# Gated recurrence: the in-chunk attention of 32-token groups as 32x32 blocks in four partition strips

## The chip, the cores and the metric

The kernel runs on one core of a Trainium2 chip. The metric is the device time of one execution in microseconds (us), lower is better. The engines are named as in the profile: PE (TensorE, matmuls), PEld (its weight loads), DVE (VectorE), ACT (ScalarE), POOL (GpSimd) and SP (SyncE, which starts the DMA transfers).

## The reference

One transformer block over 512 tokens of width 1024. A norm and one wide projection feed three branches: sparse attention with a learned index, a gated linear recurrence, and latent attention. Their outputs are gated, summed and projected, and a feed-forward part follows. The change is in the recurrence (4 heads, 128 keys and 128 values each, a decay per token and key), which the reference computes chunk by chunk like this, with `lfc` the logarithm of the decays:

```python
def step(state, xs):
    qc, kc, vc, lfc = xs
    b = jnp.cumsum(lfc, axis=2)
    o_inter = jnp.einsum('bhck,bhkv->bhcv', qc * jnp.exp(b), state)
    diff = b[:, :, :, None, :] - b[:, :, None, :, :]
    decay = jnp.exp(jnp.where(causal[None, None, :, :, None], diff, NEG_BIG))
    attn = jnp.einsum('bhtk,bhsk,bhtsk->bhts', qc, kc, decay)
    o_intra = jnp.einsum('bhts,bhsv->bhtv', attn, vc)
    b_last = b[:, :, -1:, :]
    new_state = (jnp.exp(b_last[:, :, 0, :])[..., None] * state
                 + jnp.einsum('bhsk,bhsv->bhkv', kc * jnp.exp(b_last - b), vc))
    return new_state, o_inter + o_intra
```

So a query at token t meets a key at token s <= t with the product of the decays between the two.

## The kernel before

The kernel is written as a plan. Calls such as `PE.matmul` or `V.tensor_mul` only record an instruction; `Plan.run` then orders all of them by a list schedule over the five engines, with a cost for each (`Plan.cost`), a latency between engines, an extra 500 ns ahead of a PE instruction that waits for another engine (`SLACK`), and with limits on how many tiles of a kind may be alive. Tiles are drawn from classes of slots: `g` has 37 slots of 128x512 floats, `bank` the 8 banks of PSUM. Each engine runs its own list in that order and waits for nothing but the data and the slots. A change of one instruction can therefore move others anywhere. All instructions carry the line of the emitting call, L322 (L323 after), so they are told apart by tile names.

The large projections work on float32 split into two float32r parts. They are long rows of matmuls of 128x512: `hT_hi` and `hT_lo` (the two parts of the normed input, transposed) against `whi` and `wlo`. ACT casts each weight tile `raw` to `whi`, DVE forms `wlo` from the difference. SP issues the transfers of the weights in program order. While the recurrence is computed, the list of PE alternates its blocks with such rows, for the projections of the next heads and for the gates of the branches; DVE and ACT work beside it on the bias of the sparse attention, which is chosen by a tree of selections (`mux<-bits,mux` and the like).

`hgrn_pair` computes the recurrence for two heads; it is called twice. The kernel takes chunks of 128 tokens, 4 per head. The attention tile `at` (128 keys x 4 chunks x 128 queries) is built by levels. First the diagonal, from a full 128x128 product per chunk (`pd`) times the identity. Then level hh = 1, 2, 4, ... 64: queries in the upper half of each group of 2 hh tokens meet keys in its lower half, `qT` and `kT` having been multiplied by the decays up to the middle (`tt` holds products of decays over ever longer stretches). Up to hh = 16 a level takes one 128x64 product per chunk, of which a predicated copy with the mask `ci` takes the right entries into `at`. For hh = 32 and 64 there are only narrow matmuls with outputs at their own partitions, which ACT copies into `at`. Then the keys are transposed (`kn`), the states summed (`S`), the output is formed (`bi` are the values), normed (`rb` on POOL), gated (`og`), transposed and split into `ob_hi` and `ob_lo`.

At the start of the program x is normed (`jk` on ACT with its sum of squares, `r` on POOL), transposed on PE, and cast to `hT_hi`; the first projections run row tile by row tile. A mask `cm` comes from the constants through `cw`.

Of the kernel before, what the change touches and what calls it, by code (L numbers as in the profile page):

```python
# [48 lines left out]
def _consts():  # L49
    f = np.zeros((128, 512 + 32), np.float32)  # L50
    p = np.arange(128)
    f[:, 384:512] = np.where(p[None, :] <= p[:, None], 0.0, NEG)
    f[:, 512:544] = np.array([float.fromhex(v) for v in INV_FREQ], np.float32)[None, :]
    lv = np.zeros((128, 7, 64), np.int32)
    for n in range(7):
        h = 1 << n
        s, t = p[:, None], p[p % (2 * h) >= h][None, :]
        lv[:, n] = (s // (2 * h) == t // (2 * h)) & (s % (2 * h) < h)
    return f, lv.reshape(128, 448)


class Buf:
    """A tile of the plan: one slot of its class, from its first write to its last access."""

# [7 lines left out]
class View:  # L72
    """A slice of a Buf: the elements it covers, and how to cut the slice out of the real tile."""

# [68 lines left out]
class Plan:  # L143
    """Records the instructions, then emits them in the order of a list schedule over the engines."""

# [180 lines left out]
def block_kernel(ctx: ExitStack, tc: tile.TileContext, x, positions, w_in, w_up_a, w_up_b, w_up_c, w_out, mla_q_norm,  # L326
# [25 lines left out]
    def const(shape, dt=F32, name="c"):  # L352
        v = plan.tile(nm("const"), shape, dt, name)
        slots[v.buf.cls] = [(cpool, v.buf.cls)]
        v.buf.left = 1
        return v
# [8 lines left out]

# [1 line left out]
    xt = []  # L367
# [21 lines left out]

# [1 line left out]
    class W:  # L391
        pass

    def unit(segs, kt, width, tag=""):
        """segs: (source AP [kt*128, n], column in the unit). -> hi, lo [128, kt, width]"""
        w = W()
# [39 lines left out]
    def rstd(m, n, name="r"):  # L436
        """m ** -0.5, [128, n]"""
        r = st(n, name)
        P.tensor_tensor(r, m, mhalf[:, 0:n], op=ALU.pow)
        return r  # L440

    def rms2(ss, name):
        """1/sqrt(ss[0] + ss[1] + eps)"""
        m = st(1, "ms")
        V.scalar_tensor_tensor(m, ss[:, 0:1], EPS, ss[:, 1:2], op0=ALU.add, op1=ALU.add)
        return rstd(m, 1, name)
# [9 lines left out]

# [1 line left out]
    hT = (plan.tile("hT", (8, 512), F32R, "hT_hi"), plan.tile("hT", (8, 512), F32R, "hT_lo"))  # L458

    def norm_rows(src, gain, dst, t, r=None, plain=None):  # L460
        """src: two [128, 512] halves of a row tile; transposed into columns t of dst"""
        if r is None:
# [20 lines left out]

# [1 line left out]
    va = const((4, 128,), F32, "va")  # L485
# [22 lines left out]
    def two_parts(hi, los, pt, tt):  # L508
        """pt: 64 rows twice -> hi; their low part, over or under zeros"""
        A.copy(hi[:, tt], pt)  # L510
        for e, lo in enumerate(los):
            a, b = (0, 64) if e == 0 else (64, 128)
            V.tensor_sub(lo[:, tt].part(a, b), pt.part(a, b), f32(hi[:, tt]).part(a, b))
# [58 lines left out]
    SP.dma_start(invf, consts_f[:, 512:544])  # L572
    ci = const((7, 64), I8, "ci")
    cw = g((128, 7, 64), I32, "cw")
    SP.dma_start(cw.rearrange("p a b -> p (a b)"), consts_i)
    A.copy(ci, cw)
    pos_i = const((4,), I32, "pos_i")
    SP.dma_start(pos_i, positions[0].rearrange("(a p) -> p a", p=128))
# [14 lines left out]
    rows_group([(src(C_AV, 128), 0), (src(C_IK, 72), 128), (src(C_KPE, 64), 200)], 264, put1)  # L593
# [1 line left out]
    pos_f = const((4,), F32, "pos_f")  # L595
# [17 lines left out]
    V.tensor_scalar(cs, cs, -2.0, 1.0, op0=ALU.mult, op1=ALU.add)  # L613
    # the lower bound: a softmax over the depth (one layer), its running sum less its first term
    lbe = const((4,), F32, "lbe")
# [21 lines left out]
    def rope(dst, a, heads, t):  # L637
        """a, dst: [128, heads, 64]"""
        c = cs[:, t:t + 1].to_broadcast([128, heads, 32]) if heads > 1 else cs[:, t:t + 1]
# [34 lines left out]

# [1 line left out]
    iqT = []  # L676
# [38 lines left out]
    def bias_unit(parts, heads):  # L715
        """rel_bias[bucket] by a tree of selections on the bits of the bucket; parts: (block, first column)"""
        n = sum(128 * (i + 1) for i, _ in parts)
# [58 lines left out]
    background(bias_unit, [(3, 0)], range(4))  # L776
# [1 line left out]
    SC_C = float(np.float32(192 ** -0.5))  # L778
# [45 lines left out]

# [1 line left out]
    def soft(p, i, addend=None):  # L826
        """softmax of the rows in PSUM (+ addend), transposed: [128 keys, block, 128 rows]"""
        S = 128 * (i + 1)
# [21 lines left out]
    def attend(h, logits, addend, value, dst):  # L850
        """softmax(logits + addend) @ value, transposed, in two parts"""
        ot = bank("ot")
# [24 lines left out]

# [1 line left out]
    fT, kT, qT = {}, {}, {}  # L879
# [26 lines left out]
    def hgrn_pair(hs):  # L906
        qp, at, tt_ = {}, {}, {}
        for h in hs:
            at[h] = g((128, 4, 128), name="at")
            pd = bank("t", (128, 4, 128))  # L910
            for c in range(4):
                cc = slice(c * 128, (c + 1) * 128)
                PE.matmul(pd[:, c], kT[h][:, cc], qT[h][:, cc], start=True, stop=True)
            V.tensor_mul(at[h], pd, ident.rearrange("p (a c) -> p a c", a=1).to_broadcast([128, 4, 128]))
            qp[h] = qT[h]
# [11 lines left out]
        for lv in range(7):  # L927
            hh = 1 << lv
            for h in hs:
                pl = bank("t", (128, 4, 64))  # L930
                if hh >= 32:
                    for c in range(4):
                        for s in range(0, 128, 2 * hh):
                            m = 128 * c + s
                            PE.matmul(pl[:, c, 0:hh].part(s, s + hh), kT[h][:, m:m + hh], qp[h][:, m + hh:m + 2 * hh],
                                      start=True, stop=True)
                    for s in range(0, 128, 2 * hh):
                        A.copy(at[h][:, :, s + hh:s + 2 * hh].part(s, s + hh), pl[:, :, 0:hh].part(s, s + hh))
                for c in range(4 if hh < 32 else 0):
                    cc = slice(c * 128, (c + 1) * 128)  # L940
                    q2 = qp[h][:, cc].rearrange("p (n two e) -> p n two e", two=2, e=hh)[:, :, 1]
                    PE.matmul(pl[:, c], kT[h][:, cc], q2, start=True, stop=True)
                if hh < 32:
                    a2 = at[h].rearrange("p c (n two e) -> p c n two e", two=2, e=hh)[:, :, :, 1]
                    m2 = ci[:, lv:lv + 1].to_broadcast([128, 4, 64]).rearrange("p c (n e) -> p c n e", e=hh)
                    V.copy_predicated(a2, m2, pl.rearrange("p c (n e) -> p c n e", e=hh))
                if hh == 1:
                    tv = fT[h].rearrange("p (n two) -> p n two", two=2)
                else:
                    o = 512 - 1024 // hh  # L950
                    tv = tt_[h][:, o:o + 512 // hh].rearrange("p (n two) -> p n two", two=2)
# [52 lines left out]

# [1 line left out]
    aqT = []  # L1006
# [13 lines left out]

# [1 line left out]
    mixed = [None] * 8  # L1022
# [38 lines left out]

# [1 line left out]
    mx = [(o8(name="mxh"), o8(name="mxl")) for _ in range(2)]  # L1063
# [6 lines left out]
    def acc8(hi_of, lo_of, wsrc, nk, tail):  # L1070
        """banks[half][t] = rows x columns; the last `tail` units row tile by row tile"""
        us = nk // 2
# [37 lines left out]

# [1 line left out]
    act = []  # L1112
# [13 lines left out]
    for f in range(2):  # L1126
        ffn_mm(f, [slice(0, 256)])
    # column blocks in pairs by Winograd's seven products: (block, next) x (halves of the sum) x (halves of the rows)
    lo_t, hi_t, ka, kb = slice(0, 256), slice(256, 512), slice(0, 4), slice(4, 8)

    def sums():
        """-> the four sums of blocks of h, in two parts"""
        y = [[hf[t][:, 4 * k:4 * k + 4] for t in range(2)] for k in range(2)]
# [165 lines left out]
```

## Time and profile before

| what | value |
| --- | --- |
| runs, device time | 920.32, 922.41, 922.94 us (median 922.41) |
| profiled execution, span from first to last instruction | 919.2 us |
| mean granted clock of PE | 0.995 |
| busy: PE, PEld, DVE, ACT, POOL | 904.9, 794.1, 704.6, 513.2, 19.7 us |
| share of the chain that ended last: PE, DMA, DVE, ACT | 89%, 4%, 3%, 2% |

The profile is of one execution, and its span is 3.2 us below the median of the runs; durations and starts below are of that execution. Matmuls are pipelined, so the record of one is longer than the time from its start to the next start. The busy time of an engine counts overlapped stretches once.

### The profile page before, as it was taken

How to read it: one execution, taken by the hardware profiler on the slowest of the kernel's cores; microseconds unless marked ns; L12 is line 12 of the kernel's file. 1: busy time of each engine (PE TensorE's matmuls, PEld its weight loads, DVE VectorE, ACT ScalarE, POOL GpSimd, SP SyncE). 2: the span in 40 equal slices, each digit the busy share in tenths (PEclk: the TensorE clock that was granted, in tenths of full speed). 3: DMA queues.
4: the chain of work that ended last, by engine and by line, in shares of the span. 5: the costliest groups of instructions: out<-in, count | busy, mean ns of one | idle time of the engine just before them, and what ended most of it. 6: DMA issues, size and time to landing. Idle time of an engine off the chain costs nothing.

```text
span 919.2 us, 14038 instructions
## 1 busy us (share of the span) xinstructions
PE 904.9 (98%) x5294; PEld 794.1 (86%) x5294; DVE 704.6 (77%) x1432; ACT 513.2 (56%) x958; POOL 19.7 (2%) x27
## 2 busy tenths in 40 slices
PE   8999999999999999999999999999999999999996
PEld 7998878888888888887888878999999999988885
DVE  5576999998989999999454437979998899844205
ACT  5656684494638699698932326645454545543103
POOL 1000000000111000000000000000000000000000
PEclk8999999999999999999999999999999999999999
DMA  8333122331111322324014371333334333643102
GB/s 265 86 92 98 47 70 66 95 92 47 46 58 45 105 92 75 109 92 117 23 56 128 121 221 48 96 90 92 93 93 137 93 92 116 184 138 105 56 1 91
DMA packets 76804, 86.64 MB, mean 94 GB/s; under 512 B 8257, under 2 KB 63809, under 8 KB 76737
## 3 DMA queue, kind: packets, MB, share of 16 engines
q1 hardware_dynamic: 76736, 85.76, 31.1%
q8 instruction: 41, 0.67, 0.3%
q14 instruction: 27, 0.21, 0.1%
HBM read 83.64 MB, written 2.10 MB: 93 GB/s over the span
## 4 chain that ended last, share of the span: by engine, by line
PE 89%; DMA 4%; DVE 3%; ACT 2%; issue 1%; SPq 0%; POOL 0%; POOLq 0%; ACTq 0%
PE ps L322 89%; DVE wlo L322 1%; DMA raw<-in_w_ffn_up 1%; ACT whi L322 1%; DMA x2b<-in_x 1%; DMA raw<-in_w_in 1%; DMA cw<-in_consts_f 1%; DMA raw<-in_w_out 1%; SPq L322 0%; DVE qpT L322 0%; ACT qpT L322 0%; ACT jk L322 0%; DVE qpr L322 0%; ACT hT_hi L322 0%; ACT L322 0%
## 5 line engine op out<-in xcount | busy, mean ns | idle before, releaser
L322 DVE TENSOR_TENSOR wlo<-raw,whi 128x1024 fp32r<-128x1024 f32 (+3 forms) x115 | 133.3, 1179 | 66.4 <-ACT whi L322 43.3
L322 ACT CAST whi<-raw 128x1024 fp32r<-128x1024 f32 (+3 forms) x115 | 114.8, 1015 | 90.6 <-PE ps L322 29.3
L322 PE MATMUL ps<-hT_hi,whi 128*128 128x512 f32 x328 | 130.2, 397 | 0.0
L322 PE MATMUL ps<-hT_lo,whi 128*128 128x512 f32 x328 | 130.1, 398 | 0.0
L322 PE MATMUL ps<-hT_hi,wlo 128*128 128x512 f32 x328 | 129.8, 397 | 0.0
L322 ACT ACTIVATE mux<-bucket,rb,rbd 128x512 f32<-128x512 f32 (+1 forms) x157 | 105.8, 744 | 6.4 <-DVE bucket L322 6.1
L322 DVE COPY_PREDICATED mux<-bits,mux 128x512 f32<-128x512 int8 x150 | 104.6, 751 | 0.5 <-ACT mux L322 0.5
L322 PE MATMUL ps<-tl,sh 128*128 128x256 f32 x288 | 81.5, 283 | 0.0
L322 PE MATMUL ps<-th,sl 128*128 128x256 f32 x288 | 81.5, 283 | 0.0
L322 PE MATMUL ps<-th,sh 128*128 128x256 f32 x288 | 81.5, 283 | 0.0
L322 ACT CAST sh<-sf 128x512 fp32r<-128x512 f32 x72 | 44.2, 621 | 51.4 <-DVE sf L322 29.1
L322 PEld LDWEIGHTS ps<-hT_lo,whi 128*128 128x128 f32 x328 | 61.8, 188 | 11.8
L322 PEld LDWEIGHTS ps<-hT_hi,wlo 128*128 128x128 f32 x328 | 61.7, 188 | 11.7 <-issue 0.2
L322 PEld LDWEIGHTS ps<-hT_hi,whi 128*128 128x128 f32 x328 | 61.7, 188 | 11.7
L322 PE MATMUL ps<-whi,ah 128*128 128x512 f32 x176 | 68.5, 389 | 0.0
L322 PE MATMUL ps<-wlo,ah 128*128 128x512 f32 x176 | 68.5, 389 | 0.0
L322 PE MATMUL ps<-whi,al 128*128 128x512 f32 x176 | 68.5, 389 | 0.0
L322 PE MATMUL ps<-h_hi,sl 128*128 128x256 f32 x216 | 61.1, 283 | 0.0
L322 PE MATMUL ps<-h_lo,sh 128*128 128x256 f32 x216 | 61.1, 283 | 0.0
L322 PE MATMUL ps<-h_hi,sh 128*128 128x256 f32 x216 | 61.1, 283 | 0.0
L322 PE MATMUL ps<-whi,hT_hi 128*128 128x512 f32 (+3 forms) x160 | 54.4, 346 | 1.1 <-ACT hT_hi L322 1.1
L322 PEld LDWEIGHTS ps<-th,sh 128*128 128x128 f32 x288 | 55.3, 192 | 0.0
(310 smaller groups left out, 2157.0 us busy)
## 6 DMA issues: line engine op xcount, KB each, us to landing
raw<-in_w_in SPq DMA_DIRECT2D x51, 512.0 KB, 4.3
raw<-in_w_ffn_down SPq DMA_DIRECT2D x22, 512.0 KB, 4.4
raw<-in_w_ffn_gate SPq DMA_DIRECT2D x18, 512.0 KB, 3.8
raw<-in_w_ffn_up SPq DMA_DIRECT2D x18, 512.0 KB, 4.2
raw<-in_w_out SPq DMA_DIRECT2D x8, 512.0 KB, 4.6
raw<-in_w_up_c SPq DMA_DIRECT2D x4, 512.0 KB, 3.6
raw<-in_w_up_b SPq DMA_DIRECT2D x4, 512.0 KB, 3.5
raw<-in_w_up_a SPq DMA_DIRECT2D x4, 512.0 KB, 3.8
```

Source lines behind the costliest of these rows:

```text
L322: getattr(real[e], method)(*[fix(v) for v in a], **{n: fix(v) for n, v in k.items()})
```

## The change

The levels 1 to 16 and the diagonal stay within groups of 32 tokens. After the change their products are made as 32x32 blocks (32x16 for the levels): per chunk four matmuls with 32 weight columns, each into its own strip of 32 partitions of a compact tile `ac` (32 keys in each of the four strips x 4 chunks x 32 queries). The diagonal product, the predicated copies and the mask `ci` (128x80 instead of 128x448 constants) work on `ac`, at a quarter of the width. After level 16 four ACT copies of 32x128 expand `ac` into the diagonal blocks of `at`, which POOL has set to zero. At hh = 64 the outputs of the chunks alternate between the two halves of the partitions, and two ACT copies take the place of one. A small identity `id32` is made at the start by four ACT copies. Comments and docstrings are taken out too.

```diff
--- before
+++ after
-    lv = np.zeros((128, 7, 64), np.int32)
-    for n in range(7):
+    lv = np.zeros((128, 5, 16), np.int32)
+    q = np.arange(32)
+    for n in range(5):
         h = 1 << n
-        s, t = p[:, None], p[p % (2 * h) >= h][None, :]
+        s, t = p[:, None] % 32, q[q % (2 * h) >= h][None, :]
         lv[:, n] = (s // (2 * h) == t // (2 * h)) & (s % (2 * h) < h)
-    return f, lv.reshape(128, 448)
+    return f, lv.reshape(128, 80)
...
-    ci = const((7, 64), I8, "ci")
-    cw = g((128, 7, 64), I32, "cw")
+    ci = const((5, 16), I8, "ci")
+    cw = g((128, 5, 16), I32, "cw")
     SP.dma_start(cw.rearrange("p a b -> p (a b)"), consts_i)
     A.copy(ci, cw)
+    id32 = const((1, 32), F32, "id32")
+    for i in range(4):
+        A.copy(id32[:, 0].part(32 * i, 32 * i + 32), ident[:, 32 * i:32 * i + 32].part(32 * i, 32 * i + 32))
...
     def hgrn_pair(hs):
-        qp, at, tt_ = {}, {}, {}
+        qp, at, ac, tt_ = {}, {}, {}, {}
         for h in hs:
+
             at[h] = g((128, 4, 128), name="at")
-            pd = bank("t", (128, 4, 128))
+            P.memset(at[h], 0.0)
+            ac[h] = g((128, 4, 32), name="ac")
+            pd = bank("t", (128, 4, 32))
             for c in range(4):
-                cc = slice(c * 128, (c + 1) * 128)
-                PE.matmul(pd[:, c], kT[h][:, cc], qT[h][:, cc], start=True, stop=True)
-            V.tensor_mul(at[h], pd, ident.rearrange("p (a c) -> p a c", a=1).to_broadcast([128, 4, 128]))
+                for i in range(4):
+                    m = 128 * c + 32 * i
+                    PE.matmul(pd[:, c].part(32 * i, 32 * i + 32), kT[h][:, m:m + 32], qT[h][:, m:m + 32], start=True,
+                              stop=True)
+            V.tensor_mul(ac[h], pd, id32.to_broadcast([128, 4, 32]))
...
             hh = 1 << lv
             for h in hs:
-                pl = bank("t", (128, 4, 64))
-                if hh >= 32:
+                pl = bank("t", (128, 4, 16 if hh < 32 else 64))
+                if hh == 64:
                     for c in range(4):
-                        for s in range(0, 128, 2 * hh):
+                        s, m = 64 * (c % 2), 128 * c
+                        PE.matmul(pl[:, c].part(s, s + 64), kT[h][:, m:m + 64], qp[h][:, m + 64:m + 128], start=True,
+                                  stop=True)
+                    for e in range(2):
+                        A.copy(at[h][:, e:4:2, 64:128].part(0, 64), pl[:, e:4:2].part(64 * e, 64 * e + 64))
+                elif hh == 32:
+                    for c in range(4):
+                        for s in (0, 64):
                             m = 128 * c + s
-                            PE.matmul(pl[:, c, 0:hh].part(s, s + hh), kT[h][:, m:m + hh], qp[h][:, m + hh:m + 2 * hh],
+                            PE.matmul(pl[:, c, 0:32].part(s, s + 32), kT[h][:, m:m + 32], qp[h][:, m + 32:m + 64],
                                       start=True, stop=True)
-                    for s in range(0, 128, 2 * hh):
-                        A.copy(at[h][:, :, s + hh:s + 2 * hh].part(s, s + hh), pl[:, :, 0:hh].part(s, s + hh))
-                for c in range(4 if hh < 32 else 0):
-                    cc = slice(c * 128, (c + 1) * 128)
-                    q2 = qp[h][:, cc].rearrange("p (n two e) -> p n two e", two=2, e=hh)[:, :, 1]
-                    PE.matmul(pl[:, c], kT[h][:, cc], q2, start=True, stop=True)
-                if hh < 32:
-                    a2 = at[h].rearrange("p c (n two e) -> p c n two e", two=2, e=hh)[:, :, :, 1]
-                    m2 = ci[:, lv:lv + 1].to_broadcast([128, 4, 64]).rearrange("p c (n e) -> p c n e", e=hh)
+                    for s in (0, 64):
+                        A.copy(at[h][:, :, s + 32:s + 64].part(s, s + 32), pl[:, :, 0:32].part(s, s + 32))
+                else:
+                    for c in range(4):
+                        for i in range(4):
+                            m = 128 * c + 32 * i
+                            q2 = qp[h][:, m:m + 32].rearrange("p (n two e) -> p n two e", two=2, e=hh)[:, :, 1]
+                            PE.matmul(pl[:, c].part(32 * i, 32 * i + 32), kT[h][:, m:m + 32], q2, start=True, stop=True)
+                    a2 = ac[h].rearrange("p c (n two e) -> p c n two e", two=2, e=hh)[:, :, :, 1]
+                    m2 = ci[:, lv:lv + 1].to_broadcast([128, 4, 16]).rearrange("p c (n e) -> p c n e", e=hh)
                     V.copy_predicated(a2, m2, pl.rearrange("p c (n e) -> p c n e", e=hh))
+                    if hh == 16:
+                        for i in range(4):
+                            ii = slice(32 * i, 32 * i + 32)
+                            A.copy(at[h][:, :, ii].part(32 * i, 32 * i + 32), ac[h].part(32 * i, 32 * i + 32))
...
```

The order of PE, at the first blocks of the first pair of heads (`ps<-qT,kT` is a block, with its count of matmuls; the other rows are the stream of a projection). Before:

```order
L322 MATMUL ps_2472<-qT_2461,kT_2361 128x128 x4
L322 MATMUL ps_2463<-hT_hi_137,wlo_2359 128x512
L322 MATMUL ps_2463<-hT_hi_137,whi_2342 128x512
L322 MATMUL ps_2463<-hT_lo_145,whi_2342 128x512
L322 MATMUL ps_2463<-hT_hi_137,wlo_2359 128x512
L322 MATMUL ps_2463<-hT_hi_137,whi_2342 128x512
L322 MATMUL ps_2463<-hT_lo_145,whi_2342 128x512
L322 MATMUL ps_2497<-qT_2403,kT_2315 128x64 x4
```

And after, at the same place:

```order
L323 MATMUL ps_2497<-qT_2483,kT_2374 32x32 x16
L323 MATMUL ps_2488<-hT_hi_156,wlo_2372 128x512
L323 MATMUL ps_2488<-hT_hi_156,whi_2355 128x512
L323 MATMUL ps_2488<-hT_lo_169,whi_2355 128x512
L323 MATMUL ps_2488<-hT_hi_156,wlo_2372 128x512
L323 MATMUL ps_2530<-qT_2416,kT_2328 32x16 x16
L323 MATMUL ps_2488<-hT_hi_156,whi_2355 128x512
L323 MATMUL ps_2488<-hT_lo_169,whi_2355 128x512
L323 MATMUL ps_2488<-hT_hi_156,wlo_2372 128x512
L323 MATMUL ps_2488<-hT_hi_156,whi_2355 128x512
L323 MATMUL ps_2488<-hT_lo_169,whi_2355 128x512
L323 MATMUL ps_2488<-hT_hi_156,wlo_2372 128x512
```

A block has 16 matmuls of 32 columns where it had 4 of 128, and the rows of the stream between the blocks are dealt out anew.

The order of ACT at the start of the program, before:

```order
L322 ACT_TABLE_LOAD
L322 ACTIVATE jk_104,ss_105<-xa_80 128x512
L322 ACTIVATE jk_114,ss_105<-xb_84 128x512
L322 CAST whi_128<-raw_95 128x768
L322 CAST hT_hi_137<-ps_130 128x4x128
L322 CAST whi_128<-raw_100 128x768
L322 CAST hT_hi_137<-ps_139 128x4x128
```

And after:

```order
L323 ACT_TABLE_LOAD
L323 COPY id_91_93<-ident_78 32x32 x4
L323 ACTIVATE jk_113,ss_114<-xa_80 128x512
L323 ACTIVATE jk_125,ss_114<-xb_84 128x512
L323 CAST whi_141<-raw_101 128x768
L323 CAST whi_141<-raw_109 128x768
L323 CAST hT_hi_156<-ps_143 128x4x128
L323 CAST hT_hi_156<-ps_151 128x4x128
```

The copies of the identity stand at the head, and both casts of `whi` stand ahead of the first `hT_hi`.

The order of DVE at the first levels of the first pair, before (the two heads have `at_2476` and `at_2489`):

```order
L322 COPY_PREDICATED at_2489<-ci_297,ps_2506 128x256
L322 TENSOR_TENSOR qT_2461<-qT_2461,fT_2352 128x256
L322 TENSOR_TENSOR kT_2361<-kT_2361,fT_2352 128x256
L322 COPY_PREDICATED mux_2445<-bits_2120,mux_2474 128x512
L322 COPY_PREDICATED at_2476<-ci_297,ps_2527 128x128x2
L322 TENSOR_TENSOR qT_2403<-qT_2403,tt_2325 128x128x2
L322 TENSOR_TENSOR kT_2315<-kT_2315,tt_2325 128x128x2
L322 COPY_PREDICATED at_2489<-ci_297,ps_2542 128x128x2
L322 TENSOR_TENSOR qT_2461<-qT_2461,tt_2380 128x128x2
L322 TENSOR_TENSOR kT_2361<-kT_2361,tt_2380 128x128x2
```

And after (`ac_2504` and `ac_2589`):

```order
L323 COPY_PREDICATED ac_2589<-ci_305,ps_2559 128x64
L323 COPY_PREDICATED ac_2504<-ci_305,ps_2582 128x32x2
L323 TENSOR_TENSOR qT_2416<-qT_2416,tt_2338 128x128x2
L323 TENSOR_TENSOR kT_2328<-kT_2328,tt_2338 128x128x2
L323 COPY_PREDICATED mux_2444<-bits_2133,mux_2458 128x512
L323 COPY_PREDICATED ac_2589<-ci_305,ps_2611 128x32x2
L323 TENSOR_TENSOR qT_2483<-qT_2483,tt_2393 128x128x2
L323 TENSOR_TENSOR kT_2374<-kT_2374,tt_2393 128x128x2
```

The predicated copies are of a quarter of the width, and a selection of the bias (`mux`) now stands between the two heads here.

## Rows read from the trace of the kernel before

**Rows 1.** The page's first line and its part 1.

```profile
span 919.2 us, 14038 instructions
...
PE 904.9 (98%) x5294; PEld 794.1 (86%) x5294; DVE 704.6 (77%) x1432; ACT 513.2 (56%) x958; POOL 19.7 (2%) x27
```

**Rows 2.** Busy us by stretch: PE, PEld, DVE, ACT, POOL; clock, DMA share, GB/s.

```profile
209.00:303.00 94.00, 93.97 (x636) 80.60 (x635) 83.92 (x187) 54.42 (x111) 9.55 (x4) 1.00 0.20 57
303.00:430.00 127.00, 127.00 (x565) 105.20 (x564) 125.71 (x219) 105.07 (x157) 0.00 (x0) 1.00 0.29 88
```

**Rows 3.** Whom PE waits for, 26 to 520 us: total, times, longest.

```profile
PE ps L322 <- ACT kz L322: 0.6, 1, 0.6
```

**Rows 4.** Timeline of PE around a diagonal or level block: start, duration.

```profile
213.18 0.39 PE L322 MATMUL ps<-hT_hi,whi 128*128 128x512 f32 x1
213.41 0.39 PE L322 MATMUL ps<-hT_lo,whi 128*128 128x512 f32 x1
213.64 1.00 PE L322 MATMUL ps<-qT,kT 128*128 128x64 f32 x8
214.44 0.48 PE L322 MATMUL ps<-hT_hi,wlo 128*128 128x512 f32 x1
214.76 0.39 PE L322 MATMUL ps<-hT_hi,whi 128*128 128x512 f32 x1
```

**Rows 5.** Timeline of PE around a block of level 32 (two strips).

```profile
231.58 0.40 PE L322 MATMUL ps<-hT_hi,wlo 128*128 128x512 f32 x1
231.90 0.45 PE L322 MATMUL ps<-qT,kT 128*32 128x32 f32 x16
232.28 0.50 PE L322 MATMUL ps<-hT_hi,whi 128*128 128x512 f32 x1
232.62 0.39 PE L322 MATMUL ps<-hT_lo,whi 128*128 128x512 f32 x1
232.85 0.40 PE L322 MATMUL ps<-hT_hi,wlo 128*128 128x512 f32 x1
```

**Rows 6.** Groups by form, PE, 195 to 303 us.

```profile
L322 PE MATMUL ps<-qT,kT 128*32 128x32 f32 x64 | 1.8, 199 | 0.0
```

**Rows 7.** Timeline of PE, a block of level 64 (one half strip).

```profile
237.32 0.68 PE L322 MATMUL ps<-qT,kT 128*64 128x64 f32 x8
```

**Rows 8.** Groups by form, DVE, 195 to 303 us: busy, mean ns.

```profile
L322 DVE COPY_PREDICATED mux<-bits,mux 128x512 f32<-128x512 int8 x48 | 34.0, 747 | 0.0
...
L322 DVE COPY_PREDICATED at<-ci,ps 128x256 f32<-128x256 int8 x20 | 11.1, 556 | 5.3 <-PE ps L322 5.3
...
L322 DVE TENSOR_TENSOR at<-ps,ident 128x512 f32<-128x512 f32 x4 | 2.8, 694 | 0.0
...
L322 DVE TENSOR_TENSOR tt<-tt 128x64 f32<-128x64 f32 x4 | 0.9, 223 | 0.0
```

**Rows 9.** Timeline of DVE in the levels.

```profile
227.62 0.44 DVE L322 COPY_PREDICATED at<-ci,ps 128x256 f32<-128x256 int8 x1 [0.16 <-PE ps L322]
227.96 0.42 DVE L322 TENSOR_TENSOR qT<-qT,tt 128x256 f32<-128x256 f32 x1
```

**Rows 10.** Groups by form, ACT, 195 to 303 us.

```profile
L322 ACT COPY at<-ps 32x128 f32<-32x128 f32 x8 | 2.0, 256 | 7.4 <-PE ps L322 7.3
```

**Rows 11.** Timeline of PE at the start (two stretches).

```profile
11.75 0.69 PE L322 MATMUL ps<-whi,hT_lo 128*128 128x384 f32 x1
...
25.48 0.44 PE L322 MATMUL ps<-whi,hT_hi 128*128 128x384 f32 x1 [0.22 <-ACT hT_hi L322]
```

**Rows 12.** Timeline of ACT at the start.

```profile
10.49 0.83 ACT L322 CAST whi<-raw 128x768 fp32r<-128x768 f32 x1
```

**Rows 13.** The chain that ended last, at the start: start, us.

```profile
15.20 6.58 DMA cw<-in_consts_f
...
24.94 0.49 ACT hT_hi L322
```

**Rows 14.** Groups by form, POOL.

```profile
L322 POOL MEMSET ident<- 128x128 f32 x1 | 0.2, 204 | 0.3 <-POOLq L1288 0.3
```

## The prediction

> **What bounds the kernel now.** I read the page's first part, then the busy time by stretch, then what TensorE waits for, and only then single blocks. On the page TensorE is busy for 904.9 of 919.2 us [rows 1]. The recurrence is the stretch from 209 to 303 us: TensorE is busy for 93.97 of its 94 us, VectorE for 83.9 and ScalarE for 54.4; in the 127 us behind it TensorE is busy throughout [rows 2]. Between 26 and 520 us the longest wait of TensorE sums to 0.6 us [rows 3]. So inside this stretch the queue of TensorE is the clock: the blocks of the recurrence stand between projection matmuls ("stream matmuls", 128x512), and a block costs what the stream is held up by it.
>
> The profiled span is 919.2 us and the median of the runs 922.41, 3.2 above it. I make the sum against the span's stretches and take it from the median.
>
> **What a block costs now.** The start of one stream matmul to the next is 0.23 us (213.18 to 213.41). From 213.18 to 214.76 there are three of them and one wide block, so the block costs 1.58 - 0.69 = 0.89 us [rows 4]. It has four matmuls, 8 passes in the trace, since each float32 matmul is run twice. 24 blocks are of this kind: four diagonal ones (128 rows wide instead of 64; I take them at the same price, their weights being as wide) and 20 of levels 1 to 16.
>
> **What a block costs after.** It becomes 16 matmuls, 32 passes, each with 32 columns of weights, into four strips of partitions. The trace has no block in four strips, but one in two: the level of 32, with 8 matmuls and 16 passes. From 231.58 to 232.85 there are three stream matmuls and this block: 1.27 - 0.69 = 0.58 us [rows 5]. One pass of it takes 199 ns [rows 6] and all 16 take 0.45 us, so passes follow one another by (0.45 - 0.20)/15 = 16.7 ns; about 0.58 - 16 x 0.0167 = 0.31 us is fixed, the price of going to narrow tiles and back. Against it the half-tile block of level 64, whose matmuls all use the same half, takes 0.68 us for only 8 passes [rows 7]. I read this as two strips running side by side: in the trace a pair of passes, one in each strip, comes every 33 ns.
>
> The bounds of a block of 32 passes are then:
> - four strips side by side, a set of four every 33 ns: 8 x 0.033 + 0.31 = 0.58 us;
> - two at a time as now, 16.7 ns apart: 32 x 0.0167 + 0.31 = 0.84 us;
> - no overlap, each pass as long as one strip needs in rows 5, 33 ns: 0.31 + 32 x 0.033 = 1.37 us.
>
> I take the first. In rows 5 a strip is free again every 33 ns, and nothing in the rows is shared by two strips. That gives 24 x (0.89 - 0.58) = 7.4 us. Level 64 puts its outputs on alternating halves; if its 0.68 us falls to the 0.45 of the two-strip block, that is 4 x 0.23 = 0.9 us. Sum: **8.3 us** off TensorE.
>
> The Trainium skill, page "TensorEngine Tiling (Array Packing)", section "Instruction Overhead", speaks against this: each matmul has about 60 cycles of overhead, and a tiling factor should not be taken from a dimension that is already small. An estimate by it at 2.4 GHz is 25 ns a pass, 0.31 + 32 x 0.025 = 1.11 us a block, 24 x 0.22 = 5.3 us slower. The 16.7 ns of rows 5 disagree with it for two strips; no run here shows four.
>
> **VectorE.** 20 predicated copies go from 256 to 64 columns: 556 ns busy on average, the next op 0.34 us behind its start [rows 8, 9]; an op of 64 columns is 223 ns busy against 0.42 us for one of 256, so each gives back about 0.2 us: 4 us. Four masked products of 694 ns go to a quarter of the width, 0.4 each: 1.6 us. VectorE doesn't set the end here, so this is worth nothing by itself. But the order of after draws eight more mux selections (0.75 us each [rows 8]), one leaf and four steps of bias preparation into the recurrence, some 7 us, and as many stream matmuls stay there as before (217 and 218 by the order). VectorE then has 83.9 - 5.6 + 7 = 85.3 us of busy time in a stretch of 94 - 8.3 = 85.7. That ends of ops run beside the next op's start makes it less tight: with each op at the start-to-start time of its kind, as 0.34 us for the copy of 256 columns [rows 9], I add up 78 us from the first masked product to the last output, where TensorE has 90 - 8 = 82 (first block at 213, end at 303). So VectorE still fits, with little to spare; between nothing and half of the 8.3 us given back I put **1 us** of stalls into the sum, by rows 3, where TensorE did not wait.
>
> **ScalarE.** Sixteen copies of 32x128 come in (256 ns each [rows 10], 4.1 us) and four copies of 64x256 become eight of half the size. ScalarE has 54.4 of 94 us [rows 2], so they are hidden. But the copies of one head wait for the last predicated copy, and behind them in ScalarE's queue stand the casts of the next weights and the copies that free the projection's PSUM: if level 16 is late, these are late, and next the stream. That is part of the 1 us.
>
> **GpSimd.** Four memsets of 128x512 are new. One of 128x128 takes 204 ns [rows 14], so by size four of 128x512 are at most 3.3 us. Three are ahead of the first norm's power, where GpSimd, busy for 19.7 us of the whole span [rows 1], waits for VectorE; the fourth is behind it. Hidden by that wait; if it were not there, the first norm would be up to 2.5 us later. They hold four of 37 slots of the g class until the recurrence, and yet the order of TensorE doesn't differ between the start and the recurrence, so no cost.
>
> **Start.** The four identity copies stand at the head of ScalarE, which idles for the first x tile there. The order of ScalarE then puts the second whi cast (0.83 us [rows 12]) ahead of the first hT_hi cast, so the third matmul, at 11.75 us now [rows 11], starts about 1 us later. In return the casts of the third row tile stand ahead of cm, whose wait for the constants' transfer (15.20 + 6.58 = 21.78 us) is on the chain and delays hT_hi to 24.94 [rows 13], where TensorE stalls and restarts at 25.48 [rows 11]: up to 1 us comes back. Net **0**, bounds -1 and +1.7. The smaller mask (40 KB for 224) is on that queue too, and hidden.
>
> **Sum.** -7.4 - 0.9 + 1 + 0 = -7.3, so 922.4 - 7.3 = **about 915.1 us**.
>
> **Rivals.**
> - *Strips overlap in pairs only*, so the change hardly does what it says: 0.84 us a block, 24 x 0.05 + 0.9 = 2.1 us: 920.3, no change to be told. For it: only pairs are seen in rows 5. Against: nothing in the row says that two is the limit. 0.14.
> - *VectorE or ScalarE becomes the bound of the recurrence.* VectorE's 85.3 of 85.7 us speak for it, and that a stall of TensorE is not made up later since it is full until 430 us. Against: rows 9 show VectorE waiting for TensorE in the levels. If half of the 8.3 is given back: 918.3. 0.20.
> - *The other side: 32 passes in four strips go one after another*, as a queue of matmuls that can't start them faster would have it: 33 ns each is 1.37 us a block and 24 x 0.48 = 11.5 us slower; midway to the 16.7 of rows 5, at 25 ns, it is 1.11 and 5.3 slower. So 927 to 934, and 928 the likelier end. It decides from 18 ns a pass on (0.89 - 0.31, over 32). For it: four strips are untried in these rows, and 16.7 is close to 18. Against: the 16.7 was reached with half the strips. 0.09.
>
> **Numbers.** The likeliest case has 0.57. Three runs of one kernel lie 2.6 us apart, so 0.3% (2.8 us) is about what can be told from no change. The likeliest case alone spans 912 to 918: no stall and 1 us back at the start (913), or 3 us of stalls (917), and 1 us for the runs. With VectorE's and the pairs' case the range is 911.8 to 920.6, which leaves out the slower case and the ends. Faster: the likeliest and nearly all of the VectorE case, 0.75; within 0.3%: the pairs' case and the rest, 0.16; slower 0.09.
>
> **What would show it.** In the trace of after, a block x32 of 32-column passes with about 0.58 us added to the stream (0.84 for pairs, 1.1 and over for the other side), passes about 8 ns apart; the recurrence about 8 us shorter, TensorE full in it; VectorE's wait for ps gone if VectorE is the bound, and then idle time of TensorE <- DVE or ACT, some 4 us; the third matmul near 12.8 us. The prediction is wrong if the set of four doesn't overlap, if the narrow passes have a larger fixed part than rows 5 show, or if ScalarE's order holds the stream's PSUM copies or casts behind the copies of level 16.

## The result

The changed kernel takes 912.45 us (median of 4 runs, 910.30 to 913.64), the kernel before 921.81 in the same comparison (920.32 to 922.94): a ratio of 0.9899, 95% interval 0.9882 to 0.9915, so 9.3 us faster (7.8 to 10.9). A second timing of the same program, in the experiments, gave 0.9914 (0.9899 to 0.9930).

The page of the changed kernel, as [rows 1]:

```profile
span 908.5 us, 15211 instructions
...
PE 895.1 (99%) x5870; PEld 777.6 (86%) x5870; DVE 695.6 (77%) x1428; ACT 521.5 (57%) x985; POOL 20.9 (2%) x31
```

The profiled span is 10.7 us shorter, and TensorE's busy time 9.8: the time came off TensorE. The recurrence (here and below from 0.1 us ahead of the first block to the start of the last output), before:

```profile
209.23:302.08 92.85, 92.82 (x631) 79.65 (x630) 82.77 (x186) 53.27 (x110) 9.55 (x4) 1.00 0.19 54
```

And after, with the stretch behind it, columns as in [rows 2]:

```profile
207.50:293.93 86.43, 86.40 (x1212) 65.72 (x1212) 81.43 (x198) 63.17 (x134) 8.41 (x4) 1.00 0.20 58
293.93:420.00 126.07, 126.07 (x559) 104.34 (x558) 122.42 (x211) 103.37 (x156) 0.00 (x0) 1.00 0.31 96
```

TensorE is full here as before, in 86.4 us where the recurrence took 92.85. VectorE is at 81.43 of 86.43 us, so it is closer to full than before (82.77 of 92.85), but not full.

A block of level 1 between stream matmuls, to set against [rows 4]:

```profile
212.28 0.40 PE L323 MATMUL ps<-hT_lo,whi 128*128 128x512 f32 x1
212.52 0.40 PE L323 MATMUL ps<-hT_hi,wlo 128*128 128x512 f32 x1
212.84 0.44 PE L323 MATMUL ps<-qT,kT 128*32 128x16 f32 x32
213.22 0.50 PE L323 MATMUL ps<-hT_hi,whi 128*128 128x512 f32 x1
213.55 0.40 PE L323 MATMUL ps<-hT_lo,whi 128*128 128x512 f32 x1
```

There are three stream matmuls of 0.23 us and the block between 212.28 and 213.55: 1.27 - 0.69 = 0.58 us. The same reckoning over all blocks that stand between stream matmuls has a median of 0.577 us (19 of them), against 0.896 before (20). The 32 passes are recorded in 0.44 us, as long as the 16 of [rows 5].

The groups by form, for the level blocks and for level 64:

```profile
L323 PE MATMUL ps<-qT,kT 128*32 128x16 f32 x640 | 8.9, 185 | 0.0
...
L323 PE MATMUL ps<-qT,kT 128*64 128x64 f32 x32 | 1.8, 234 | 0.0
```

In the same reckoning a block of level 64 costs 0.69 us against 0.86 before (two such blocks in each trace). And the whole list of TensorE's waits from 26 to 700 us:

```profile
PE ps L323 <- ACT kz L323: 0.6, 1, 0.6
PE ps L323 <- ACT whi L323: 0.5, 1, 0.5
PE ps L323 <- ACT pT L323: 0.3, 1, 0.3
```

None of them is in the recurrence. The wait for `whi` lies near 530 us and was 1.6 us in the profiled execution of the kernel before; ScalarE waited there for a transfer.

The start, against [rows 11]: ScalarE's first weight cast before and after, then two stream matmuls on TensorE after (the first and the third):

```profile
9.27 0.83 ACT L322 CAST whi<-raw 128x768 fp32r<-128x768 f32 x1 [4.12 <-DMA raw<-in_w_in]
...
8.34 0.83 ACT L323 CAST whi<-raw 128x768 fp32r<-128x768 f32 x1 [3.28 <-DMA raw<-in_w_in]
```

```profile
10.76 0.69 PE L323 MATMUL ps<-whi,hT_hi 128*128 128x384 f32 x1 [1.45 <-ACT hT_hi L323]
...
11.87 0.69 PE L323 MATMUL ps<-whi,hT_lo 128*128 128x384 f32 x1
```

The third matmul starts at 11.87, not at 12.8; but the first weights were there 0.9 us earlier in this execution (8.34 against 9.27), and that doesn't come from the change, as the experiments show.

### The profile page after: what moved, and what is told of

The parts are those of the page before. It is cut to its first block, busy times and chain, and to the rows that moved or that the text cites. A ratio compares the mean times of both kernels' runs of the same rounds, so it can differ in the third digit from the quotient of the medians.

```text
span 908.5 us, 15211 instructions
## 1 busy us (share of the span) xinstructions
PE 895.1 (99%) x5870; PEld 777.6 (86%) x5870; DVE 695.6 (77%) x1428; ACT 521.5 (57%) x985; POOL 20.9 (2%) x31
## 4 chain that ended last, share of the span: by engine, by line
PE 92%; DMA 3%; DVE 2%; ACT 1%; issue 1%; SPq 0%; POOLq 0%; POOL 0%; ACTq 0%
PE ps L323 92%; DMA raw<-in_w_ffn_up 1%; DMA raw<-in_w_in 1%; DVE wlo L323 1%; DMA x2b<-in_x 1%; ACT whi L323 1%; DMA raw<-in_w_out 1%; SPq L323 0%; DVE qpT L323 0%; ACT qpT L323 0%; ACT L323 0%; DVE ckT_lo L323 0%; ACT sm L323 0%; DVE kpo L323 0%; DVE qpr L323 0%
## 5 line engine op out<-in xcount | busy, mean ns | idle before, releaser
L323 ACT ACTIVATE mux<-bucket,rb,rbd 128x512 f32<-128x512 f32 (+1 forms) x161 | 108.3, 743 | 11.0 <-DVE bucket L323 4.7
```

The source lines that it names most:

```text
L323: getattr(real[e], method)(*[fix(v) for v in a], **{n: fix(v) for n, v in k.items()})
```

## The experiments

Ratios are to the kernel before on the same chip, whose median was 920.2 to 920.5 us there; the changed kernel stands at 0.9899 and 0.9914, about 912 us. "A block" is always the price in the stream, as above.

**Strip by strip.** The same matmuls in another order within a block (the diagonal likewise):

```diff
-                    for c in range(4):
-                        for i in range(4):
+                    for i in range(4):
+                        for c in range(4):
```

> The changed kernel, but each block issues the four matmuls of one strip in a row, then those of the next strip (same matmuls, same count, same place in TensorE's list). If strips run side by side and one strip needs 33 ns per pass, a pass now waits for its own strip: 32 x 33 ns + 0.31 = 1.37 us a block instead of 0.58, 24 x 0.79 = 19 us slower than the changed kernel, about 931 us, and TensorE still full. If narrow passes are simply short, whatever their strip, a block stays at 0.58 us and the time at that of the changed kernel (912 us).

It took 922.98 us, ratio 1.0030 (1.0019 to 1.0041): 11 us slower than the changed kernel, and 0.3% slower than the kernel before. TensorE around a block:

```profile
213.06 0.40 PE L323 MATMUL ps<-hT_hi,wlo 128*128 128x512 f32 x1
213.39 0.88 PE L323 MATMUL ps<-qT,kT 128*32 128x16 f32 x32
214.20 0.50 PE L323 MATMUL ps<-hT_hi,whi 128*128 128x512 f32 x1
214.54 0.39 PE L323 MATMUL ps<-hT_lo,whi 128*128 128x512 f32 x1
```

From 213.06 to 214.54 there are two stream matmuls and the block: 1.48 - 0.46 = 1.02 us, and the median over the blocks is 1.017. 24 x 0.44 = 10.6 us is the whole loss. The single records inside it show passes of one strip 32 ns apart, and the first passes of the next strip running beside the last ones of the strip before. So neither expected price came: the first one (1.37 us) left out that strips overlap at the seams. What it settles: a strip takes a pass every 32 ns, strips run side by side, and the gain hangs on the order in which the 16 matmuls are issued.

**Two strips at a time.**

```diff
-                    for c in range(4):
-                        for i in range(4):
+                    for c, i in [(c, i + j) for i in (0, 2) for c in range(4) for j in range(2)]:
```

> The changed kernel, but a block issues its matmuls in alternation over strips 0 and 1 and then over strips 2 and 3, so that only two strips run side by side, apart from the seam between the halves. Sets of two every 32 ns: 16 x 0.032 + 0.31 = 0.82 us, less up to 0.1 at the seam, so 0.72 to 0.82 a block against 0.58: 24 x 0.14 to 0.24 = 3.4 to 5.8 us slower than the changed kernel. If the number of strips at a time doesn't matter, no change.

915.51 us, ratio 0.9947 (0.9934 to 0.9961): 3.7 us slower than the changed kernel, inside what was expected.

```profile
212.38 0.40 PE L323 MATMUL ps<-hT_hi,wlo 128*128 128x512 f32 x1
212.71 0.59 PE L323 MATMUL ps<-qT,kT 128*32 128x16 f32 x32
213.23 0.50 PE L323 MATMUL ps<-hT_hi,whi 128*128 128x512 f32 x1
213.57 0.39 PE L323 MATMUL ps<-hT_lo,whi 128*128 128x512 f32 x1
```

The block is 1.19 - 0.46 = 0.73 us (median 0.724): 24 x 0.147 = 3.5 us. That is less than the 0.84 of the prediction's pairs, since the two halves overlap at their seam here.

**Blocks twice.** The first try named the buffers wrongly (they carry a number), so that nothing was issued twice: it is the changed kernel again.

```diff
...
+            run()
+            if method == "matmul" and a[1].buf.name == "kT" and a[1].idx.size == 32 and a[0].buf.shape[-1] < 64:
+                done = blocks.setdefault(a[0].buf, [])
+                done.append(run)
+                if len(done) == 16:
+                    for again in done:
+                        again()
```

(`run` issues the instruction at hand.)

> The changed kernel, but each of the 24 blocks issues its 16 matmuls twice (same result, all else in the same order). It separates the fixed part of a block from that of a pass. With 0.31 us fixed and a set of four passes every 33 ns, a block goes from 0.58 to 0.84 us and the time rises by 24 x 0.26 = 6.3 us, to about 919. If 0.58 us is a floor of going to narrow tiles and back, in which more passes are free, nothing changes. If a pass costs 17 ns or more at the margin, it is 13 us or more.

912.51 us, ratio 0.9914 (0.9899 to 0.9930). Its use is a second profile of the changed kernel. ScalarE's first weight cast, then on TensorE the first stream matmul and the first block:

```profile
9.52 0.83 ACT L324 CAST whi<-raw 128x768 fp32r<-128x768 f32 x1 [4.52 <-DMA raw<-in_w_in]
```

```profile
11.95 0.69 PE L324 MATMUL ps<-whi,hT_hi 128*128 128x384 f32 x1 [1.50 <-ACT hT_hi L324]
...
208.90 0.46 PE L324 MATMUL ps<-qT,kT 128*32 128x32 f32 x32
```

Here the weights came at 9.52, close to the 9.27 of the kernel before. The first stream matmul is 1.3 us later than before (10.64), and the first block all the same 0.4 us earlier (209.33): the stall of [rows 13] is gone.

With the name mended (`startswith("kT_")`):

> The changed kernel, but each of the 24 blocks issues its 16 matmuls twice in four strips (same result, all else in the same order). The run before shows that strips run side by side and one strip takes a pass every 32 ns. If a block is 0.31 us fixed and 8 sets of four passes, the doubled one has 16 sets: 0.58 + 8 x 0.032 = 0.84 us, 24 x 0.26 = 6.2 us slower than the changed kernel. If 0.58 us is a floor of going to narrow tiles and back, in which more passes are free, nothing changes; at 17 ns a pass or more it is 13 us or more slower.

923.90 us, ratio 1.0039 (1.0025 to 1.0053): 12 us slower than the changed kernel, twice what was expected.

```profile
213.49 0.40 PE L324 MATMUL ps<-hT_hi,wlo 128*128 128x512 f32 x1
213.82 0.74 PE L324 MATMUL ps<-qT,kT 128*32 128x16 f32 x64
214.48 0.51 PE L324 MATMUL ps<-hT_hi,whi 128*128 128x512 f32 x1
214.82 0.40 PE L324 MATMUL ps<-hT_lo,whi 128*128 128x512 f32 x1
```

A block of 64 passes is 1.33 - 0.46 = 0.87 us (median 0.877), 0.30 more than one of 32: 24 x 0.30 = 7.2 us, which answers to sets of four some 37 ns apart and a fixed part near 0.29. The rest is a wait that no other kernel here has:

```profile
PE ps L324 <- issue: 3.4, 7, 1.0
```

Seven times TensorE had nothing to issue, in the middle of blocks, 3.4 us by this view and 4.7 by the gaps between starts. 7.2 + 4.7 = 11.9. The trace points to what was missing: the instructions themselves. From one of these waits to the next TensorE has 256 records, give or take one, or a multiple of that (five times and three times; matmul passes, weight loads and its sequencer's records are counted). And each wait ended 2.2 to 2.4 us after the start of a transfer of 16 KB on a DMA queue that the profile calls "instruction"; that queue moved 15 such packets between 205 and 308 us, against 9 in the changed kernel between 205 and 294.

**The start alone**, on the kernel before:

```diff
     A.copy(ci, cw)
+    id32 = const((1, 32), F32, "id32")
+    for i in range(4):
+        A.copy(id32[:, 0].part(32 * i, 32 * i + 32), ident[:, 32 * i:32 * i + 32].part(32 * i, 32 * i + 32))
...
             at[h] = g((128, 4, 128), name="at")
+            P.memset(at[h], 0.0)
```

> The kernel before with two parts of the change alone: the four identity copies on ScalarE and the four memsets of the attention tiles on GpSimd (whose results are not needed there). The order of ScalarE at the start is then that of the changed kernel, the blocks are the old ones. If the earlier start of the changed kernel's recurrence (207.6 us against 209.3) comes from this order, the recurrence starts at about 207.6 here too and the time is 1.7 us below the kernel before, about 920. If it came from transfers that happened to land earlier in that one execution, no change: 921.8.

920.27 us, ratio 0.9999 (0.9990 to 1.0008): no change. TensorE's first stream matmul and first block:

```profile
12.07 0.69 PE L322 MATMUL ps<-whi,hT_hi 128*128 128x384 f32 x1 [1.42 <-ACT hT_hi L322]
...
209.12 0.94 PE L322 MATMUL ps<-qT,kT 128*128 128x128 f32 x7
```

The first is 1.4 us later than before, the second 0.2 earlier. So the order at the start is worth about nothing, and the 207.6 of the changed kernel's profile was the early transfer: the same program started its recurrence at 208.9 when the weights came at 9.52. (It is the memsets that change ScalarE's order: with the identity copies alone the planner keeps the casts where they were.)

**TensorE's part alone.** The kernel before in its own order, 16 narrow matmuls for each level block, VectorE's copies as wide as before:

```diff
+            b = [fix(v) for v in a]
+            if method == "matmul" and a[1].buf.name.startswith("kT_") and a[1].idx.size == 128 and a[2].idx.size == 64:
+                o, kk, q = b
+                w = int(q.shape[1]) // 4
+                for i in range(4):
+                    real[e].matmul(o[32 * i:32 * i + 32, 0:16], kk[:, 32 * i:32 * i + 32], q[:, w * i:w * i + w],
+                                   **{n: fix(v) for n, v in k.items()})
+                continue
+            if method == "copy_predicated" and a[0].buf.name.startswith("at_"):
+                b[2] = a[2].buf.real[:, :, 0:1].to_broadcast([128, 4, 64]).rearrange(...)
...
```

> The kernel before, in its own order on every engine, but each of the 20 level blocks is issued as 16 narrow matmuls in four strips, with the predicated copies as wide as before (they read one value per key and chunk for the whole row, so the entries of the levels are not the right ones). It is TensorE's part alone: 20 x 0.31 = 6.2 us less for blocks. If TensorE alone sets the pace, all of it shows: about 6 us faster than the kernel before. If VectorE's work must shrink too, as the run with its copies done three times suggests (VectorE is busy for 83.9 us, and 92.7 - 6.2 = 86.5 us would be left), part of it is given back as waits of TensorE for VectorE: 2 to 4 us faster.

912.35 us, ratio 0.9910 (0.9897 to 0.9924): 8.2 us faster (7.0 to 9.5), as fast as the whole change. The recurrence (first block to last output), columns as in [rows 2]:

```profile
208.83:295.35 86.52, 86.47 (x1111) 67.17 (x1110) 81.77 (x186) 53.33 (x110) 9.56 (x4) 1.00 0.21 59
```

It is 6.3 us shorter than before, 20 x 0.32, and TensorE is full: nothing is given back, though VectorE does its old work (its 20 copies take 550 ns each, against 556). That the time fell by some 2 us more than the recurrence is not settled. The stretches before and behind it, whose order did not change, were shorter than in the profiled execution of the kernel before (by 0.4 and 2.1 us), and the one behind was so too in the next kernel (by 1.9), which was at most 2 us faster. Of these 2.1 us, 1.6 can be TensorE's wait for `whi` near 540 us: it is 1.6 us in that profile and not listed in these two, and in the profiles of all the other kernels here it lies anywhere from 0.5 to 1.6.

**VectorE's part alone.** The kernel before in its own order, predicated copies of a quarter of the width:

```diff
+            if method == "copy_predicated" and a[0].buf.name.startswith("at_"):
+                a = [v[:, 0:1] for v in a]
```

> The kernel before, in its own order on every engine, but its 20 predicated copies take only the first of the four chunks, 64 columns instead of 256 (the entries of the other three chunks are left out). It is VectorE's part of the change alone: 20 x 0.2 = 4 us less VectorE work, the blocks still wide. If TensorE was the bound before, by its own blocks, nothing changes (within 1 us of the kernel before). If VectorE's work in the levels had a part in the pace already then, 2 to 4 us faster.

919.92 us, ratio 0.9990 (0.9981 to 0.9999): under 2 us, and nothing in the recurrence:

```profile
210.11:302.96 92.85, 92.81 (x630) 79.63 (x629) 77.16 (x186) 53.26 (x110) 9.56 (x4) 1.00 0.18 54
```

VectorE is at 77.16 us, 5.6 below the kernel before (82.77), and the recurrence is as long as before (92.85 in both). Twenty copies got shorter by 298 ns of busy time each (258 against the 556 of [rows 8]); that is idle time now.

**VectorE's work put back** into the changed kernel, each predicated copy three times or twice, order unchanged:

```diff
+            for again in range(3 if method == "copy_predicated" and a[0].buf.name.startswith("ac_") else 1):
+                getattr(real[e], method)(*[fix(v) for v in a], **{n: fix(v) for n, v in k.items()})
```

> The changed kernel, but VectorE does each of its 20 quarter-width predicated copies three times (same result, same order on all engines): about 40 x 0.14 = 5.6 us of VectorE work put back, as much as the change took away, with the blocks still short. If TensorE alone sets the recurrence and VectorE has a few us to spare, the time moves by less than 1 us. If VectorE is close to being the bound there, as the second rival had it, up to 3 to 5 us come back as waits of TensorE for VectorE.

> The changed kernel, but each predicated copy is done twice instead of three times: 20 more copies. Three times cost 9 us with 9.1 us of VectorE's busy time more in the recurrence. If the time followed the added work from the first microsecond, half of it costs 4.5 us. If VectorE first had a reserve (it is busy for 81.4 of 86.4 us in the changed kernel), these 4.6 us cost clearly less, 0 to 2 us, and the price sets in behind that.

Three times: 920.56 us, ratio 1.0009 (1.0000 to 1.0017), the whole gain lost. Twice: 914.87 us, ratio 0.9935 (0.9923 to 0.9948), 3 us lost. The recurrence with copies done twice, and then three times:

```profile
208.34:297.24 88.90, 87.36 (x1212) 65.66 (x1212) 85.42 (x219) 63.12 (x134) 8.34 (x4) 1.00 0.20 57
```

```profile
209.60:304.02 94.42, 88.27 (x1212) 66.03 (x1212) 90.54 (x239) 63.25 (x134) 8.28 (x4) 1.00 0.18 53
```

VectorE's busy time goes from 81.4 to 85.4 and 90.5 us, the recurrence from 86.4 to 88.9 and 94.4. The first 4 us cost 2.5, the next 5.1 cost 5.5. With three times TensorE waits in the recurrence:

```profile
PE ps L324 <- DVE kT L324: 3.5, 10, 0.7
PE ps L324 <- DVE ac L324: 1.4, 3, 0.6
PE ps L324 <- ACT at L324: 0.7, 2, 0.4
```

So there is a small reserve, and behind it the time follows VectorE one to one.

**The expanding copies twice**, in the changed kernel, order unchanged:

```diff
+            wide = method == "copy" and a[0].buf.name.startswith("at_") and a[1].buf.name.startswith("ac_")
+            for again in range(2 if wide else 1):
...
```

> The changed kernel, but ScalarE makes each of the 16 copies that expand the compact tile twice (same result, same order): about 16 x 0.2 = 3 us more ScalarE work at the end of the levels, ahead of the weight casts and PSUM copies that are queued behind it. If these copies are hidden, as the sum had it, no change. If they hold back the stream of TensorE, up to 3 us, with waits of TensorE for ScalarE in the recurrence.

918.62 us, ratio 0.9987 (0.9975 to 0.9999): 7 us slower than the changed kernel, more than either case. TensorE's wait in the recurrence, and the second of the two places in stretches of 2 us:

```profile
PE ps L325 <- ACT at L325: 3.9, 2, 2.0
```

```profile
272.00:274.00 2.00, 2.00 (x15) 1.36 (x14) 1.88 (x5) 1.89 (x6) 0.00 (x0) 1.00 0.10 36
274.00:276.00 2.00, 0.06 (x1) 0.01 (x1) 0.73 (x1) 1.93 (x6) 0.00 (x0) 1.00 0.00 0
276.00:278.00 2.00, 1.97 (x13) 1.66 (x14) 0.63 (x2) 1.95 (x5) 0.00 (x0) 0.53 0.00 0
278.00:280.00 2.00, 2.00 (x11) 1.77 (x9) 2.00 (x4) 1.43 (x4) 0.00 (x0) 0.61 0.00 0
```

Twice TensorE waits 2.0 us for `at`. Behind the second wait (TensorE busy for 0.06 of the 2 us to 276) the granted clock is 0.53 and 0.61, that is mostly the lower level of 1.2 GHz, for some 3.5 us at half speed: 1.7 us more. 3.9 + 1.7 = 5.6, and the recurrence is 92.2 us instead of 86.4. In the changed kernel itself ScalarE's copies at that place (the last row is two copies of level 32 and two of level 64, for the first head), and TensorE's first matmul that reads `at`:

```profile
264.06 1.20 ACT L323 COPY at<-ac 32x128 f32<-32x128 f32 x4
...
265.95 1.22 ACT L323 COPY at<-ac 32x128 f32<-32x128 f32 x4
...
269.00 1.10 ACT L323 COPY at<-ps 32x128 f32<-32x128 f32 x4
```

```profile
270.06 0.38 PE L323 MATMUL ps<-bi,at 128*128 128x128 f32 x2
```

The expanding copies are done at 267.17, but the copies of levels 32 and 64 stand behind them in ScalarE's queue. The last of these ends at 270.10, and the matmul, which needs `at` only in part, starts at 270.06, with no wait: it is just in time. With the expanding copies doubled, these last copies end at 276.17, and the matmul starts at 276.03, behind its wait.

**Both heads' blocks side by side**, in the changed kernel (the diagonal likewise):

```diff
         for lv in range(7):
             hh = 1 << lv
+            pls = {}
             for h in hs:
+                plan.gate = both if h == hs[0] else None
...
+            for h in hs:
+                pl = pls[h]
...
+            both = plan.ops[-1]
```

`both` is the last multiplication for the second head, so the first head's block waits for it, and all copies and multiplications of a level are recorded behind both blocks.

> The changed kernel, but the blocks of the two heads of a pair are issued back to back at the diagonal and at every level (the first head's block waits until the second's operands are there too), so TensorE goes to narrow tiles and back 16 times instead of 32. If the fixed 0.31 us is the price of going there and back, 16 x 0.31 = 5 us are saved less what levels 32 and 64 share less of: 4 to 5 us faster than the changed kernel, about 908. If the fixed part belongs to each block, no change. If the longer level makes TensorE wait, since both heads' VectorE work now lies between two blocks, it is slower, with waits of TensorE for VectorE in the recurrence.

908.63 us, ratio 0.9876 (0.9862 to 0.9890): 11.4 us faster than the kernel before, and 3.9 us below the second timing of the changed kernel, which ran beside it on the same chip. A pair of blocks:

```profile
213.75 0.39 PE L323 MATMUL ps<-hT_hi,whi 128*128 128x512 f32 x1
214.07 0.74 PE L323 MATMUL ps<-qT,kT 128*32 128x16 f32 x64
214.73 0.50 PE L323 MATMUL ps<-hT_lo,whi 128*128 128x512 f32 x1
215.07 0.39 PE L323 MATMUL ps<-hT_hi,wlo 128*128 128x512 f32 x1
```

The pair costs 1.32 - 0.46 = 0.86 us (median 0.859) where two blocks cost 1.15: 0.29 us less for each way to narrow tiles and back that is saved. Over 12 pairs of diagonal and low levels that is 3.5 us, with levels 32 (0.83 for the pair against 1.15) and 64 (0.83 against 1.38) 5.2; some 1.3 us of it are not in the time. It is the fastest version here.

## Why the prediction held, and where it didn't

The forecast was 915.1 us, 7.3 faster, in a range of 911.8 to 920.6; measured were 912.45 and 9.3 faster (7.8 to 10.9). The likeliest case is the one that came.

- *TensorE bounds the recurrence by its blocks.* Right. VectorE's part alone shortens nothing in the recurrence, TensorE's alone shortens it by all of its 6.3 us.
- *A block falls from 0.89 to 0.58 us, four strips side by side, sets of four every 33 ns.* Right: 0.577, sets every 32 ns in the single records of the trace. The runs strip by strip (1.017) and with two strips (0.724) show that it is the strips side by side that make it so, and the doubled block and the paired one that about 0.29 us are fixed. The gain is 24 x 0.32 = 7.7 against 7.4. The Trainium skill, page "TensorEngine Tiling (Array Packing)", section "Instruction Overhead", gives each matmul a fixed overhead; the prediction's estimate by it, with the overhead paid pass after pass, was 1.11 us a block. The trace disagrees with that estimate: 32 passes are recorded in 0.44 us. Within one strip passes do stand 32 ns apart; it is from strip to strip that they overlap.
- *Level 64 gives 0.9.* Mis-sized: 0.17 a block, 0.7. Together 8.4 against 8.3.
- *1 us of stalls.* Somewhat too large: no wait of TensorE is listed in the recurrence. It became 92.85 - 86.43 = 6.4 us shorter and not 8.4, since six more stream matmuls stand in it (239 against 233 in the traces, 1.4 us, which are missing behind; the prediction had counted as many as before), and 0.6 us remain for all stalls and seams. By the trace the change is thus worth 6.4 + 1.4 = 7.8 us, and by the second timing 7.9, where the forecast was 7.3. The 9.3 of the first timing is partly luck as far as its profile tells: that execution, the fastest of the four, has 1.7 us ahead of the first block from the early transfer, and waits 1.1 us less for `whi`. Whether the other three had the same is not shown.
- *VectorE's relief is worth nothing by itself, and it still fits with little to spare.* Right in both halves, with a number for "little": 81.4 of 86.4 us, and the first 4 us of more work already cost 2.5. The prediction had 85.3 of 85.7 by busy time and 78 of 82 by starts; the latter was the better measure, though it put the first block at 213, and it starts at 209.33. The rival of VectorE as the bound did not come, but the changed order stands near it: the whole gain goes with 9 us more on VectorE.
- *ScalarE's sixteen copies are hidden.* Right, but not for the reason given. ScalarE's share (54.4 of 94) says nothing about the end of the levels, where the copies stand ahead of what the output's first matmul needs: ScalarE's queue is just in time there, and when these copies take twice as long, 7 us are lost.
- *The start is worth 0, bounds -1 and +1.7.* Right: 0.2 and 0.4 earlier at the first block, in two profiles with the weights at their usual time. The third matmul did start about 1 us later there (13.06 in the second profile of the changed kernel, with weights 0.25 later), and that was made up. The 1.7 us in the first profile of the changed kernel came from an earlier transfer and would have been wrongly credited to the order.
- *Memsets and slots cost nothing.* Right, as to time; but it is the memsets that make the planner reorder ScalarE's start.
- *The other side, passes one after another.* It did not come, but the kernel strip by strip shows how near it is: the same 16 matmuls in the other loop order are slower than the kernel before.

## What to carry to other kernels

Narrow matmuls into column strips pay when consecutive ones go to different strips: the order of the loop over strips decided between 0.58 and 1.02 us a block here. The way to narrow tiles and back costs about 0.3 us each time, so blocks that can stand side by side should. Where a planner fills a shortened stretch with other work, the engines that were off the path lose their reserve: look at the places where a short engine queue meets the bound (here the copies at the end of the levels), not at shares of the span.

## What was not expected of the hardware

- With every block doubled, it looks as if TensorE used its instructions up faster than they were loaded: there are seven waits, up to 1.0 us long, about 256 of its records or a multiple apart, and each ends 2.2 to 2.4 us after a 16 KB transfer of the instruction queue has started. With 32 passes to a block there are none, nor in the kernel with pairs, which also has 64 narrow passes in a row but half as many in all.
- One wait of 2.0 us with TensorE idle was followed by about 4 us in which the granted clock was 0.53 to 0.61; a first wait of 1.9 us, 43 us earlier, was not followed by a fall (1.00 in the stretches around it).
